# Scores of the windowed attentions: the second query tile and the doubled key rows are made on chip by ScalarE instead of being loaded

## The chip, the cores and the metric

The kernel runs on one core of a Trainium2 chip. The metric is device time in microseconds (us) of one execution. Before the change the median of three runs is 1516.51 us (1511.09 to 1520.24).

## The reference, cut to what matters

Two layers of a decoder for 1024 prompt tokens and 32 decode tokens. Layer 0 has four windowed attentions of 8 query heads on 2 key heads (kv) each: A, with a sink logit, and B in three groups with dilations 1, 4 and 16, which are merged by their softmax denominators. Each prompt attention is blocked: 128 queries read their own and the previous block of 128 keys. Layer 1 is an mLSTM and is not touched.

```python
s = jnp.einsum('nbqhgd,nbkhd->nbhgqk', qb, kk, preferred_element_type=F32)
...
p, den, lse = _softmax_stats(s, mask, sink_b)      # row maximum, exp(s - max), sums
o = jnp.einsum('nbhgqk,nbkhd->nbqhgd', p, vv.astype(F32))
o = o / jnp.moveaxis(den, -1, 2)[..., None]
```

## The kernel before

Every float32 product is made of parts: a number is split into a high part h, which TensorE multiplies at full rate, and a low part l, the rest. A projection is three matmuls (h·h, l·h and h·l, L199 to L201). For the scores the head dimension is 64 and TensorE takes 128 rows at once, so the three products fit into two matmuls: L466 multiplies the key tile K1 (128 rows: h above h) with the query tile Q1 (128 rows: l above h), and L467 adds the key tile K2 (65 rows: l, and a row of ones) with Q2 (65 rows: h, and a row with minus the softmax maximum).

The tiles are laid out for that in DRAM. `proj_q` stores a group's queries in QQ as rows l (0 to 63), h (64 to 127) and the row of minus the maximum (128), so that Q1 is rows 0 to 127 and Q2 rows 64 to 128: two loads for 256 queries of four heads, 512 KB and 260 KB (L354, L369). `proj_kv` stores keys three times in KK: h, h, l, so that K1 is 128 rows and K2 the last 64 (`k1_load`, `k2_load`). For dilations 4 and 16 a key tile is first loaded into the staging tile kt, of which there is one, and VectorE permutes it into K1 or K2 (L382, L395). Q1, Q2, K1 and K2 have two buffers each.

An attention runs in two passes over four "halves" of 256 queries. The statistics pass (`stats`, L437, L441) takes row maxima of h·h from QZ, a query tile whose lower 64 rows are zero. The score pass (`scores`) makes, block by block, two score matmuls, an exponential on ScalarE (p, L469), a mask on GpSimd, a high and a low part (ph on ScalarE, pl on VectorE or GpSimd) and three matmuls with the values (L489 to L491). There are 100 such blocks in 32 halves: 8 halves of A and 24 of B.

Work is woven: the statistics and scores of A with the projections of the other queries, the statistics of the last group and the first scores of B with the gate path (`proj_z0`), and the rest of B with the decode attention and the merges. Inside that, a scheduler at build time decides the order on each engine, which then runs it strictly in that order; on the load queue (SP) too, where an issue that waits holds back all later ones.

Of the kernel before, what the change touches and what calls it, by code (L numbers as in the profile page):

```python
# [4 lines left out]
F32 = mybir.dt.float32  # L5
F32R = mybir.dt.float32r
AF = mybir.ActivationFunctionType
# [5 lines left out]
TP, TS, T = 1024, 32, 1056  # L13
CH = ((0, 384), (384, 384), (768, 288))
DIL = (1, 1, 4, 16)
# [7 lines left out]
def f(ap):  # L23
    return ap.bitcast(F32)
# [73 lines left out]
class Builder:  # L98
# [118 lines left out]
    def proj_q(self, g):  # L217
        nc = self.nc
        dil = DIL[g]
        QQ = self.QQ[g]  # L220
        for j in range(4):
            sh = self.stage.tile([128, T], F32R, tag="sh", name="sh")
            sl = self.stage.tile([128, T], F32R, tag="sl", name="sl")
            qs = self.stage.tile([128, TS], F32, tag="qs", name="qs")

            def evac(c, t0, n, ps):
                src = ps
                if j == 3:
                    rr = self.tmp.tile([128, 384], F32, tag="rr", name="rr")
                    self.rope(rr[:, :n], ps, t0, n)  # L230
                    src = rr[:, :n]
                if c == 2:
                    nc.scalar.activation(qs, src[:, 256:288], AF.Copy, scale=0.125)  # L233
                    n = 256
                a, b = t0 // dil, (t0 + n) // dil

                def pv(ap):
                    if dil == 1:
                        return ap[:, t0:t0 + n]
                    return ap[:, :TP].rearrange("p (r n) -> p n r", r=dil)[:, a:b, :]  # L240

                s = src[:, :n]
                if dil > 1:
                    s = s.rearrange("p (n r) -> p n r", r=dil)
                self.hi(pv(sh), s, 0.125)
                self.lo(pv(sl), s, pv(sh), 0.125)

            yield from self.proj_feat(self.A['w0f'][4 + 4 * g + j], self.X0, evac)
            r0 = 128 * ((j + 1) % 4)
            self.store('q', QQ[512 + r0:640 + r0, :], f(sh[:, :TP]))  # L250
            self.store('q', QQ[r0:r0 + 128, :], f(sl[:, :TP]))
            self.store('q', self.QS[g, r0:r0 + 128, :], qs)

    def proj_kv(self):
        nc, A, O = self.nc, self.A, self.O
        tc = self.tc
        with tc.tile_pool(name="kvp", bufs=1) as kp, tc.tile_pool(name="kvt", bufs=2) as kt:
# [36 lines left out]
            for j in range(4):  # L294
                sh = self.stage.tile([128, T], F32R, tag="sh", name="sh")
                sl = self.stage.tile([128, T], F32R, tag="sl", name="sl")
                self.hi(sh[:, :TP], KF[:, j, :TP])
                self.lo(sl[:, :TP], KF[:, j, :TP], sh[:, :TP])
                r0 = 128 * ((j + 1) % 4)
                for u in range(2):  # L300
                    self.store('k', self.KK[512 * u + r0:512 * u + r0 + 128, :], f(sh[:, :TP]))
                self.store('k', self.KK[1024 + r0:1152 + r0, :], f(sl[:, :TP]))
                self.store('k', self.KS[r0:r0 + 128, :], KF[:, j, TP:T])
            wv = []
            for k in range(0, 8, 2):
# [51 lines left out]
    def qh_load(self, g, kv, hf):  # L357

        Q = self.QZ[hf % 2]
        t = slice(256 * hf, 256 * hf + 256)  # L360
        h = slice(4 * kv, 4 * kv + 4)
        self.store("Qh", f(Q[0:64]), self.QQ[g].rearrange("(d h) t -> d h t", h=8)[64:128, h, t])
        return Q

    def q2_load(self, g, kv, hf):
        Q2 = self.qp.tile([65, 4, 256], F32R, tag="Q2", name="Q2")
        t = slice(256 * hf, 256 * hf + 256)
        h = slice(4 * kv, 4 * kv + 4)
        self.load(f(Q2), self.QQ[g].rearrange("(d h) t -> d h t", h=8)[64:129, h, t])  # L369
        return Q2  # L370

    def k1_load(self, g, kv):
        nc = self.nc
        dil = DIL[g]
        src = self.KK.rearrange("(d h) t -> h d t", h=8)[2 * g + kv][0:128]
        K1 = self.kp.tile([128, TP], F32R, tag="K1", name="K1")
        if dil == 1:
            self.load(f(K1), src)
        else:
            kt = self.kp.tile([128, TP], F32, tag="kt", name="kt", bufs=1)  # L380
            self.load(kt, src)
            nc.vector.tensor_copy(K1.rearrange("p (r n) -> p n r", r=dil), kt.rearrange("p (n r) -> p n r", r=dil))  # L382
        return K1

    def k2_load(self, g, kv):
        nc = self.nc
        dil = DIL[g]
        src = self.KK.rearrange("(d h) t -> h d t", h=8)[2 * g + kv][128:192]
        K2 = self.kp.tile([65, TP], F32R, tag="K2", name="K2")
        if dil == 1:  # L390
            self.load(f(K2[0:64]), src)
        else:
            kt = self.kp.tile([128, TP], F32, tag="kt", name="kt", bufs=1)
            self.load(kt[0:64], src)
            nc.vector.tensor_copy(K2[0:64].rearrange("p (r n) -> p n r", r=dil),  # L395
                                  kt[0:64].rearrange("p (n r) -> p n r", r=dil))
        nc.gpsimd.memset(f(K2[64:65]), 1.0)
        return K2

    def v_load(self, g, kv):  # L400

# [21 lines left out]

    def stats(self, g, kv, hf, Q1, K1, ST):
        nc = self.nc
        for qb in range(2 * hf, 2 * hf + 2):
# [5 lines left out]
            for hp in range(2):  # L432
                st = self.pp.tile([128, 2, 256], F32, tag=STATS_PS[hp], name="st")
                for u in range(2):
                    h = 2 * hp + u
                    q0 = 128 * (qb % 2)
                    nc.tensor.matmul(st[:, u, :], Q1[:, h, q0:q0 + 128], K1[:, w0:w0 + 256], start=True, stop=True)  # L437
                for u in range(2):
# [14 lines left out]

    def scores(self, g, kv, hf, Q1, Q2, K1, K2, V, emit):
        nc = self.nc
# [65 lines left out]

    def attn_a(self, kv):
        nc = self.nc
        K1, K2, V = self.k1_load(0, kv), self.k2_load(0, kv), self.v_load(0, kv)
        ST = self.sm.tile([128, 32], F32, tag="ST", name="ST")
        for hf in range(4):
            Q1 = self.qh_load(0, kv, hf)
            yield from self.stats(0, kv, hf, Q1, K1, ST)
        nc.vector.tensor_tensor(ST, ST, self.sinkb[:, 32 * kv:32 * kv + 32], OP.max)
        nm = self.QQ[0][1024 + 4 * kv:1028 + 4 * kv]  # L530
        self.neg_rows(ST, nm)
        OD = self.odp.tile([65, 4, TP], F32, tag="OD", name="OD")

        def emit(qb, av):
            nc.vector.tensor_copy(self.od_view(OD, 0, qb), self.av_view(av[0:65], 0))

        for hf in range(4):
            Q1 = self.q1_load(0, kv, hf)
            Q2 = self.q2_load(0, kv, hf)
            yield from self.scores(0, kv, hf, Q1, Q2, K1, K2, V, emit)  # L540
        self.store('o', self.OD[0][kv], OD)
        self.finish(0, kv, nm)

    def attn_b_stats(self, g, kv):
        K1 = self.k1_load(g, kv)
        ST = self.sm.tile([128, 32], F32, tag="ST", name="ST")
        for hf in range(4):
            Q1 = self.qh_load(g, kv, hf)
            yield from self.stats(g, kv, hf, Q1, K1, ST)
        self.neg_rows(ST, self.NMB[kv][g - 1])  # L550
# [19 lines left out]
    def attn_b(self, kv, done=None):  # L570

        nc = self.nc
        OD = self.odp.tile([65, 4, TP], F32, tag="OD", name="OD")
        for g in (3, 2, 1):
            K1, K2, V = self.k1_load(g, kv), self.k2_load(g, kv), self.v_load(g, kv)

            def emit(qb, av, g=g):
                o = self.od_view(OD, g, qb)
                a = self.av_view(av[0:65], g)
                if g == 3:  # L580
                    for s in range(2):
                        nc.vector.tensor_copy(o[:, :, s, :], a[:, :, s, :])
                else:
                    nc.vector.tensor_tensor(o, a, o, OP.add)
                if g == 1 and qb in (2, 5, 7):
                    t = slice(CH[qb // 3][0], 128 * qb + 128)
                    self.store('o', self.OD[1][kv][:, :, t], OD[:, :, t])
                    if done:
                        done(qb // 3)

            for hf in range(4):
                Q1 = self.q1_load(g, kv, hf)
                Q2 = self.q2_load(g, kv, hf)
                yield from self.scores(g, kv, hf, Q1, Q2, K1, K2, V, emit)
        if kv == 0:
            self.finish(1, kv)
# [292 lines left out]
    def layer0(self):  # L889
        nc, tc, A, O = self.nc, self.tc, self.A, self.O  # L890
        dp = self.dram
        dt = lambda n, s: dp.tile(s, F32, name=n)
# [1 line left out]
        self.QQ = [dt(f"QQ{g}", [129 * 8, TP]) for g in range(4)]  # L894
        self.QS = dt("QS", [4, 512, TS])

        self.KK, self.KS = dt("KK", [3 * 512, TP]), dt("KSd", [512, TS])

        self.VV = dt("VV", [TP, 8 * 128])
        self.NMB = [[dt(f"NMB{i}{g}", [4, TP]) for g in range(3)] for i in range(2)]  # L900
# [722 lines left out]
```

## Time and profile before

| | |
|---|---|
| runs | 1511.09, 1516.51, 1520.24 us |
| profiled execution | 1514.5 us, of which the span of the core is 1512.8 |
| TensorE (PE) busy | 1409.6 us, 93% |
| VectorE (DVE) busy | 897.7 us, 59% |
| ScalarE (ACT) busy | 472.9 us, 31% |
| GpSimd (POOL) busy | 276.4 us, 18% |
| moved by DMA | 241.01 MB, mean 159 GB/s |
| mean granted TensorE clock | 0.971 |

The shares are averages over stages. TensorE is nearly full in the projections and in layer 1, and has its holes between 440 and 700 us, where the scores of B, the decode attention and the merges run; there the DMA engines are at their busiest. An idle engine in that table therefore says little on the stage that the change touches.

### The profile page before, as it was taken

What the parts mean: (1) busy time and instruction counts of PE and PEld (TensorE: products, weight loads), DVE (VectorE), ACT (ScalarE), POOL (GpSimd) and SP (SyncE); (2) the same over time, 40 slices, a digit from 0 to 9 for tenths busy, and PEclk for the clock granted to TensorE, in tenths of its full rate; (3) what the DMA queues carried; (4) which work ended last, traced back from release to release, by engine and by line L of the source; (5) the groups of instructions that cost most, each with busy time, mean ns of one, the idle gap of its engine ahead of it and who ended that gap; (6) DMA issues with size and microseconds to landing.
All of it is one profiled execution on the core that took longest, in us unless ns stands there. A gap on an engine that the chain in (4) does not pass through costs nothing.

```text
span 1512.8 us, 21927 instructions
## 1 busy us (share of the span) xinstructions
PE 1409.6 (93%) x7792; PEld 1193.2 (79%) x7792; DVE 897.7 (59%) x2479; ACT 472.9 (31%) x892; POOL 276.4 (18%) x351
## 2 busy tenths in 40 slices
PE   8999999999988777978999999999999999999997
PEld 7989998998887434456879878988898899877785
DVE  5311556677655856758774536555565566566786
ACT  5331143521112654512124313331333133323310
POOL 1002252512334874401000000000000000000010
PEclk9999999999999978989999999999999999999999
DMA  8646665667747998894312565364224312341731
GB/s 304 222 150 209 212 187 184 188 199 202 205 135 183 226 228 179 260 273 137 128 51 72 193 222 178 97 217 135 70 78 124 116 49 68 118 127 28 239 133 46
DMA packets 149323, 241.01 MB, mean 159 GB/s; under 512 B 17632, under 2 KB 115904, under 8 KB 148696
## 3 DMA queue, kind: packets, MB, share of 16 engines
q1 hardware_dynamic: 141150, 218.24, 49.0%
q10 hardware_dynamic: 8064, 21.37, 3.9%
q8 instruction: 62, 1.02, 0.3%
q14 instruction: 47, 0.39, 0.1%
HBM read 178.66 MB, written 83.97 MB: 174 GB/s over the span
## 4 chain that ended last, share of the span: by engine, by line
PE 67%; DMA 18%; DVE 7%; issue 3%; ACT 1%; POOL 1%; SPq 1%; DVEq 0%; POOLq 0%; ACTq 0%
PE pj L199 10%; PE pj L200 10%; PE pj L201 10%; PE py L167 3%; PE py L165 3%; PE py L166 3%; PE pvo L165 3%; PE pvo L166 3%; PE pvo L167 3%; DMA G<-GR 2%; DMA Q<-QQ 2%; DMA NMB<-NM 1%; DMA QZ<-QQ 1%; DMA OD<-OD 1%; PE av L489 1%
## 5 line engine op out<-in xcount | busy, mean ns | idle before, releaser
L199 PE MATMUL pj<-x1h,wh 128*128 128x384 f32 (+1 forms) x576 | 189.7, 329 | 1.7 <-ACT QT L1156 1.6
L199 PE MATMUL pj<-xh,wh 128*128 128x384 f32 (+1 forms) x576 | 187.9, 326 | 1.2 <-DVE rt L214 1.2
L201 PE MATMUL pj<-x1h,wl 128*128 128x384 f32 (+1 forms) x576 | 187.8, 326 | 0.0
L201 PE MATMUL pj<-xh,wl 128*128 128x384 f32 (+1 forms) x576 | 187.6, 326 | 0.0
L200 PE MATMUL pj<-xl,wh 128*128 128x384 f32 (+1 forms) x576 | 187.6, 326 | 0.0
L200 PE MATMUL pj<-x1l,wh 128*128 128x384 f32 (+1 forms) x576 | 187.6, 326 | 0.0
L199 PEld LDWEIGHTS pj<-x1h,wh 128*128 128x128 f32 x576 | 108.7, 189 | 6.5 <-issue 3.3
L201 PEld LDWEIGHTS pj<-x1h,wl 128*128 128x128 f32 x576 | 108.6, 188 | 6.0 <-issue 5.8
L199 PEld LDWEIGHTS pj<-xh,wh 128*128 128x128 f32 x576 | 109.8, 191 | 4.4 <-DVE rt L214 2.2
L200 PEld LDWEIGHTS pj<-x1l,wh 128*128 128x128 f32 x576 | 108.6, 189 | 4.0 <-issue 3.8
L201 PEld LDWEIGHTS pj<-xh,wl 128*128 128x128 f32 x576 | 110.0, 191 | 1.4
L200 PEld LDWEIGHTS pj<-xl,wh 128*128 128x128 f32 x576 | 109.6, 190 | 1.1
L441 DVE CUSTOM_DVE_ANT_0 junk<-st,maskq 128x256 f32<-128x256 f32 (+1 forms) x256 | 93.0, 363 | 25.0 <-PE st L437 5.9
L165 PE MATMUL pvo<-voh,x1h 128*128 128x512 f32 x256 | 101.7, 400 | 2.5 <-DVE SZ L1172 2.5
L166 PE MATMUL pvo<-voh,x1l 128*128 128x512 f32 x256 | 100.8, 396 | 0.0
L167 PE MATMUL pvo<-vol,x1h 128*128 128x512 f32 x256 | 100.3, 395 | 0.0
L811 POOL TENSOR_TENSOR rsw<-rsw,mhalf 128x1 f32<-128x1 f32 (+1 forms) x54 | 40.2, 745 | 321.4 <-DVE rsw L810 305.6
L122 POOL TENSOR_TENSOR wl<-wr,wh 128x1024 fp32r<-128x1024 f32 x24 | 59.2, 2470 | 122.5 <-ACT qs L233 77.8
L116 DVE TENSOR_TENSOR pl<-p,ph 128x512 fp32r<-128x512 f32 x82 | 68.3, 842 | 21.7 <-ACT ph L112 15.8
L112 ACT ACTIVATE wh<-wr 128x1024 fp32r<-128x1024 f32 x48 | 50.7, 1057 | 81.5 <-PE pj L200 75.2
L112 ACT ACTIVATE ph<-p 128x512 fp32r<-128x512 f32 x100 | 61.4, 629 | 41.6 <-PE av L490 26.2
L469 ACT ACTIVATE p<-sc 128x512 f32<-128x512 f32 x100 | 56.8, 593 | 44.6 <-PE sc L467 29.1
(349 smaller groups left out, 3145.3 us busy)
## 6 DMA issues: line engine op xcount, KB each, us to landing
Q<-QQ SPq DMA_DIRECT2D x32, 512.0 KB
out_kvs_dram<-in_cache_b_kv_dram SPq DMA_DIRECT2D x16, 1022.0 KB
wr<-in_w0f_dram SPq DMA_DIRECT2D x24, 512.0 KB
wr<-in_w1f_dram SPq DMA_DIRECT2D x24, 512.0 KB
Q<-QQ SPq DMA_DIRECT2D x32, 260.0 KB
QQ<-sh ACTq DMA_DIRECT2D x16, 512.0 KB
QQ<-sl ACTq DMA_DIRECT2D x16, 512.0 KB
QZ<-QQ SPq DMA_DIRECT2D x32, 256.0 KB
```

The lines of the kernel that those rows point to most:

```text
L112: return self.nc.scalar.activation(out, in_, AF.Copy, scale=scale)
L116: return self.nc.vector.tensor_tensor(out, in_, f(hi), OP.subtract)
L122: self.nc.gpsimd.tensor_tensor(out, in_, f(hi), OP.subtract)
L165: nc.tensor.matmul(ps, xh[:, k, t], wh, start=k == 0, stop=False)
L166: nc.tensor.matmul(ps, xl[:, k, t], wh, start=False, stop=False)
L167: nc.tensor.matmul(ps, xh[:, k, t], wl, start=False, stop=k == 7)
L199: nc.tensor.matmul(ps[:, :n], wh[:, k, :], xh[:, k, :n], start=k == 0, stop=False)
L200: nc.tensor.matmul(ps[:, :n], wh[:, k, :], xl[:, k, :n], start=False, stop=False)
L201: nc.tensor.matmul(ps[:, :n], wl[:, k, :], xh[:, k, :n], start=False, stop=k == 7)
L441: nc.vector.tensor_tensor_reduce(junk[:, :n], st[:, u, c0:c0 + n], mk, 1.0, -3e38, OP.add, OP.max, ST[:, 8 * h + qb:8 * h + qb + 1])
L469: nc.scalar.activation(p, sc, AF.Exp)
L811: nc.gpsimd.tensor_tensor(r, v, self.mhalf[:m], OP.pow)
```

## The change

1. QQ holds h in rows 0 to 63 and l in rows 64 to 127. Q1 is h above l.
2. Q2 is no longer loaded: only its row 64 (minus the maximum, 4 KB) is; rows 0 to 63 are copied by ScalarE from rows 0 to 63 of Q1, which hold h (32 copies of 64x1024).
3. KK holds h and l once each. K1's rows 0 to 63 are loaded and ScalarE copies them into rows 64 to 127 (14 copies of 64x1024, of which 6 for statistics passes). For dilations 4 and 16 one load of kt brings both parts, and VectorE permutes 64 rows into K1 and, for a score pass, 64 into K2.

```diff
-            self.store('q', QQ[512 + r0:640 + r0, :], f(sh[:, :TP]))
-            self.store('q', QQ[r0:r0 + 128, :], f(sl[:, :TP]))
+            self.store('q', QQ[r0:r0 + 128, :], f(sh[:, :TP]))
+            self.store('q', QQ[512 + r0:640 + r0, :], f(sl[:, :TP]))
...
-                for u in range(2):
-                    self.store('k', self.KK[512 * u + r0:512 * u + r0 + 128, :], f(sh[:, :TP]))
-                self.store('k', self.KK[1024 + r0:1152 + r0, :], f(sl[:, :TP]))
+                self.store('k', self.KK[r0:r0 + 128, :], f(sh[:, :TP]))
+                self.store('k', self.KK[512 + r0:640 + r0, :], f(sl[:, :TP]))
...
-        self.load(f(Q2), self.QQ[g].rearrange("(d h) t -> d h t", h=8)[64:129, h, t])
+        self.load(f(Q2[64:65]), self.QQ[g].rearrange("(d h) t -> d h t", h=8)[128:129, h, t])
+        self.nc.scalar.activation(Q2[0:64], f(Q1[0:64]), AF.Copy)
...
-    def k1_load(self, g, kv):
+    def k_load(self, g, kv, low=True):
...
+        K2 = self.kp.tile([65, TP], F32R, tag="K2", name="K2") if low else None
         if dil == 1:
-            self.load(f(K1), src)
+            self.load(f(K1[0:64]), src[0:64])
+            if low:
+                self.load(f(K2[0:64]), src[64:128])
         else:
+            n = 128 if low else 64
             kt = self.kp.tile([128, TP], F32, tag="kt", name="kt", bufs=1)
...
+            self.load(kt[:n], src[:n])
+            for u, d in enumerate((K1[0:64], K2[0:64]) if low else (K1[0:64],)):
+                nc.vector.tensor_copy(d.rearrange("p (r n) -> p n r", r=dil),
+                                      kt[64 * u:64 * u + 64].rearrange("p (n r) -> p n r", r=dil))
+        nc.scalar.activation(K1[64:128], f(K1[0:64]), AF.Copy)
+        if low:
+            nc.gpsimd.memset(f(K2[64:65]), 1.0)
+        return K1, K2
```

ScalarE's order in the scores of B, at the turn from dilation 16 to dilation 4 of the second key head, before. p is the exponential, ph the high part:

```order
L469 ACTIVATE p<-sc 128x512 x2
L112 ACTIVATE ph<-p 128x512 x3
L469 ACTIVATE p<-sc 128x512
L112 ACTIVATE ph<-p 128x512
L469 ACTIVATE p<-sc 128x512 x3
L112 ACTIVATE ph<-p 128x512 x3
```

And now, at the same turn. Q_5404, Q_5484 and Q_5805 are the Q2 tiles of three halves that follow each other, Q_5402, Q_5482 and Q_5803 their Q1 tiles, K_6019 the K1 of the group after:

```order
L465 ACTIVATE p<-sc 128x512 x3
L370 ACTIVATE Q_5404<-Q_5402 64x1024
L112 ACTIVATE ph<-p 128x512 x3
L465 ACTIVATE p<-sc 128x512 x2
L112 ACTIVATE ph<-p 128x512
L370 ACTIVATE Q_5484<-Q_5482 64x1024
L465 ACTIVATE p<-sc 128x512
L370 ACTIVATE Q_5805<-Q_5803 64x1024
L465 ACTIVATE p<-sc 128x512
L112 ACTIVATE ph<-p 128x512
L391 ACTIVATE K_6019<-K_6019 64x1024
```

Copies stand between the exponentials of earlier halves. Each waits for its half's two loads; what stands behind it on ScalarE waits too.

The load queue (SP) at the first scores of B, before (Q with 65 rows is Q2, with 128 rows Q1):

```order
L106 DMA Q_4174<-QQ_78 65x4x256
L106 DMA Q_4242<-QQ_78 65x4x256
L106 DMA wr<-in_wo_dram 128x1024
L106 DMA kt<-KK 64x1024
L106 DMA Q_4328<-QQ_78 128x4x256
L106 DMA Q_4330<-QQ_78 65x4x256
L106 DMA kt<-KK 128x1024
L106 DMA Q_4396<-QQ_78 128x4x256
```

And now:

```order
L106 DMA Q_4185<-QQ_78 1x4x256
L106 DMA Q_4254<-QQ_78 1x4x256
L106 DMA wr<-in_wo_dram 128x1024
L106 DMA kt<-KK 128x1024
L106 DMA Q_4341<-QQ_78 128x4x256
L106 DMA Q_4343<-QQ_78 1x4x256
L106 DMA Q_4410<-QQ_78 128x4x256
```

The loads keep their places; those of Q2 shrink to one row, and of the two loads of kt for a group one is left.

## Rows read from the trace of the kernel before

**Rows 1.** Busy time by stretch: PE, PEld, DVE, ACT, POOL, clock, DMA share, GB/s.

```profile
440.00:640.00 200.00, 158.97 (x692) 99.92 (x694) 133.49 (x257) 92.25 (x178) 108.61 (x132) 0.88 0.84 208
150.00:325.00 175.00, 172.00 (x1015) 159.97 (x1014) 104.74 (x282) 66.57 (x119) 63.85 (x52) 0.99 0.60 187
...
550.00:575.00 25.00, 15.94 (x41) 8.33 (x40) 9.40 (x17) 9.77 (x18) 13.46 (x27) 0.68 0.99 217
```

**Rows 2.** Waits, 440 to 640 us: who for whom, us, times, longest.

```profile
ACT p L469 <- PE sc L467: 26.0, 14, 4.8
...
DVE K L395 <- DMA kt<-KK: 12.9, 3, 5.1
...
PE sc L466 <- DMA Q<-QQ: 9.4, 5, 2.9
...
PE sc L467 <- DMA Q<-QQ: 8.8, 9, 3.4
...
DVE dn L519 <- DMA dn<-OD: 6.4, 1, 6.4
```

**Rows 3.** Chain that ended last, 435 to 600 us: start, us, what.

```profile
435.67 4.42 DMA kt<-KK
...
447.54 1.83 DMA nr<-NMB
...
469.24 4.28 DMA kt<-KK
...
481.33 4.53 DMA nr<-NMB
...
536.26 11.82 DMA Q<-QQ
...
553.11 9.79 DMA OD<-OD
562.91 12.76 DMA dn<-OD
```

**Rows 4.** DMA issues, whole span: count, KB each.

```profile
Q<-QQ SPq DMA_DIRECT2D x32, 512.0 KB
...
Q<-QQ SPq DMA_DIRECT2D x32, 260.0 KB
...
KK<-sh SPq DMA_DIRECT2D x8, 512.0 KB
...
kt<-KK SPq DMA_DIRECT2D x8, 512.0 KB
...
K<-KK SPq DMA_DIRECT2D x6, 512.0 KB
```

**Rows 5.** The same view, 480 to 640 us: packets, and loads of Q2.

```profile
DMA packets 30380, 36.33 MB, mean 227 GB/s; under 512 B 2377, under 2 KB 27127, under 8 KB 30369
...
Q<-QQ SPq DMA_DIRECT2D x20, 260.0 KB
```

**Rows 6.** ScalarE's groups by form, whole span: busy us, mean ns, idle before.

```profile
L469 ACT ACTIVATE p<-sc 128x512 f32<-128x512 f32 x100 | 56.8, 593 | 44.6 <-PE sc L467 29.1 <-DVE pl L116 12.1 <-POOL pl L485 2.3
L112 ACT ACTIVATE wh<-wr 128x1024 fp32r<-128x1024 f32 x48 | 50.7, 1057 | 81.5 <-PE pj L200 75.2 <-DMA QZ<-QQ 3.6 <-DMA wr<-in_w1f_dram 2.6
```

**Rows 7.** Timeline, 540 to 550 us: PE, then ACT: start, us, what, [idle before].

```profile
545.51 0.80 PE L466 MATMUL sc<-Q,K 128*128 128x512 f32 x1 [2.94 <-DMA Q<-QQ]
...
548.12 1.22 PE L467 MATMUL sc<-Q,K 65*128 65x512 f32 x2
...
543.04 1.08 ACT L469 ACTIVATE p<-sc 128x512 f32<-128x512 f32 x2
544.00 0.64 ACT L112 ACTIVATE ph<-p 128x512 fp32r<-128x512 f32 x1
549.44 0.60 ACT L469 ACTIVATE p<-sc 128x512 f32<-128x512 f32 x1 [4.80 <-PE sc L467]
```

More of the change, by code (lines that the diff above doesn't have):

```diff
@@ L361, in qh_load, with q2_load @@
         h = slice(4 * kv, 4 * kv + 4)
-        self.store("Qh", f(Q[0:64]), self.QQ[g].rearrange("(d h) t -> d h t", h=8)[64:128, h, t])
+        self.store("Qh", f(Q[0:64]), self.QQ[g].rearrange("(d h) t -> d h t", h=8)[0:64, h, t])
         return Q
-    def q2_load(self, g, kv, hf):
+    def q2_load(self, g, kv, hf, Q1):
         Q2 = self.qp.tile([65, 4, 256], F32R, tag="Q2", name="Q2")
@@ L368, in q2_load @@
         h = slice(4 * kv, 4 * kv + 4)
-        self.load(f(Q2), self.QQ[g].rearrange("(d h) t -> d h t", h=8)[64:129, h, t])
+        self.load(f(Q2[64:65]), self.QQ[g].rearrange("(d h) t -> d h t", h=8)[128:129, h, t])
+        self.nc.scalar.activation(Q2[0:64], f(Q1[0:64]), AF.Copy)
         return Q2
-    def k1_load(self, g, kv):
+    def k_load(self, g, kv, low=True):
         nc = self.nc
         dil = DIL[g]
-        src = self.KK.rearrange("(d h) t -> h d t", h=8)[2 * g + kv][0:128]
+        src = self.KK.rearrange("(d h) t -> h d t", h=8)[2 * g + kv]
         K1 = self.kp.tile([128, TP], F32R, tag="K1", name="K1")
+        K2 = self.kp.tile([65, TP], F32R, tag="K2", name="K2") if low else None
         if dil == 1:
-            self.load(f(K1), src)
+            self.load(f(K1[0:64]), src[0:64])
+            if low:
+                self.load(f(K2[0:64]), src[64:128])
         else:
+            n = 128 if low else 64
             kt = self.kp.tile([128, TP], F32, tag="kt", name="kt", bufs=1)
[L381 to L398, printed above, removed]
+            self.load(kt[:n], src[:n])
[6 more added lines that the diff above has]
+        return K1, K2
     def v_load(self, g, kv):
@@ L523, in attn_a @@
         nc = self.nc
-        K1, K2, V = self.k1_load(0, kv), self.k2_load(0, kv), self.v_load(0, kv)
+        (K1, K2), V = self.k_load(0, kv), self.v_load(0, kv)
         ST = self.sm.tile([128, 32], F32, tag="ST", name="ST")
@@ L538, in attn_a @@
             Q1 = self.q1_load(0, kv, hf)
-            Q2 = self.q2_load(0, kv, hf)
+            Q2 = self.q2_load(0, kv, hf, Q1)
             yield from self.scores(0, kv, hf, Q1, Q2, K1, K2, V, emit)
@@ L544, in attn_b_stats @@
     def attn_b_stats(self, g, kv):
-        K1 = self.k1_load(g, kv)
+        K1 = self.k_load(g, kv, False)[0]
         ST = self.sm.tile([128, 32], F32, tag="ST", name="ST")
@@ L574, in attn_b @@
         for g in (3, 2, 1):
-            K1, K2, V = self.k1_load(g, kv), self.k2_load(g, kv), self.v_load(g, kv)
+            (K1, K2), V = self.k_load(g, kv), self.v_load(g, kv)
             def emit(qb, av, g=g):
@@ L592, in attn_b @@
                 Q1 = self.q1_load(g, kv, hf)
-                Q2 = self.q2_load(g, kv, hf)
+                Q2 = self.q2_load(g, kv, hf, Q1)
                 yield from self.scores(g, kv, hf, Q1, Q2, K1, K2, V, emit)
@@ L895, in layer0 @@
         self.QS = dt("QS", [4, 512, TS])
-        self.KK, self.KS = dt("KK", [3 * 512, TP]), dt("KSd", [512, TS])
+        self.KK, self.KS = dt("KK", [2 * 512, TP]), dt("KSd", [512, TS])
         self.VV = dt("VV", [TP, 8 * 128])
```

## The prediction

> **What bounds the kernel now.** I read the busy time by stretch first. In the scores of A, which run beside projections, TensorE is busy 172.00 of 175 us: nothing is to be won there but by taking work from TensorE itself, and the change takes none. From 440 to 640 us, the scores of B, it is busy 158.97 of 200 us at a clock of 0.88. No other compute engine is full there: VectorE 133, GpSimd 109, ScalarE 92 of 200 us; the DMA engines stand at 0.84 over the stretch, and at 0.99 from 550 to 575, where the clock is 0.68 and ScalarE works 9.77 of 25 us [rows 1]. So the holes, 200 - 159 = 41 us, are where the change can act.
>
> Next the waits of that stretch. TensorE itself stands 9.4 + 8.8 = 18.2 us before score matmuls because a query tile has not landed: five times for Q1 (L466), nine for Q2 (L467). ScalarE in turn waits 26.0 us for L467. VectorE stands 12.9 us before a permuting copy of the second part of a key tile (L395), which needs a second load of kt, and 6.4 us before the denominators [rows 2]. The chain of waits shows what lies on the path: two loads of kt (4.42 and 4.28 us), a load of Q2 that takes 11.82 us, and, where the output tile OD passes from the first key head to the second, a store of 9.79 us and a load of the denominators of 12.76 us [rows 3]. A small transfer shows that this is largely the queue ahead of it: the 16 KB load of nr takes 1.83 us at 447.5 us and 4.53 us at 481.3 [rows 3]. The timeline shows how one late Q2 spreads: Q1's matmul starts at 545.51 after an idle 2.94 us, Q2's at 548.12, and ScalarE, done at 544.64, begins again at 549.44 [rows 7].
>
> **The change part by part.** *Bytes removed.* Each of 32 Q2 loads loses 256 of its 260 KB (8.4 MB), each of 14 K1 loads 256 KB (3.7 MB), and four of eight 512 KB stores of the high keys go (2.1 MB): 14.2 of 241 MB [rows 4]. What counts is the full stretch, 480 to 640 us: 36.33 MB at a mean of 227 GB/s. There 20 Q2 loads lose 5.2 MB and four key tiles 1.0 MB [rows 5], together 6.3 MB, 17%, or 6.3 MB / 227 GB/s = 28 us of transfer. That is the upper bound, if the transfers alone set the pace; the lower is nothing, if they run beside other work.
>
> *Waits for Q1.* Five, 9.4 us. Q1 stays 512 KB, but what is queued before it is a sixth less. A load that transits in about 6 us comes about 1 us earlier; five waits lose 1 us each: -5 us. The ends are 0 and -9.4.
>
> *Waits for Q2.* Nine, 8.8 us, the longest 3.4. Q2 is now ready when Q1 has landed and ScalarE has copied it. No row has a 64x1024 copy; the nearest is ScalarE's 128x1024 of the weights, the same 1024 elements per row, at 1057 ns [rows 6], against 593 ns for 512 elements. I take 1.06 us for a copy. In the timeline Q2 came 548.12 - 545.51 = 2.6 us after Q1 [rows 7]; a copy makes that about 1.2 us with its hand-over. Short waits stay as they are, long ones shrink: -3 us, between 0 and -8.8.
>
> *The kt wait.* For dilations 4 and 16 one load of 512 KB brings both parts, so VectorE's wait inside a group goes: 12.9 us in three, of which two, 4.42 + 4.28 = 8.7 us, lie on the chain [rows 2, 3]. What is late next is the statistics work standing there on VectorE and TensorE, and the new copy into K1's lower half, one of 1.06 us per group, behind VectorE's. I take -5 us, between 0 and -8.7.
>
> *The hand-over of OD.* 9.79 + 12.76 = 22.5 us of transfers that wait in the same queue [rows 3]. A sixth of it is 3.8 us: I take -3, between 0 and -6.
>
> *Added to ScalarE.* 32 + 14 copies of 1.06 us are 49 us in the whole span, some 25 of them (20 of Q2, four or five of K1) in the stretch, where ScalarE goes from 92 to 117 us of 200 [rows 1]. It is not full then, but the copies stand between exponentials, and each waits for two loads; behind it wait the exponentials and high parts of older blocks, behind these GpSimd's masks, VectorE's low parts and TensorE's value matmuls. Today ScalarE often stands there in any case, for the very Q loads (26.0 us) [rows 2]. I take +6 us: a quarter of the 25 us shows on the path. The ends are 0, if all of it falls into ScalarE's idle time, and +30, if every copy and half a microsecond of waiting with it does.
>
> *The rest.* The copies of A and of the statistics passes are covered by TensorE's projections, 172 of 175 us, since ScalarE has 66.57 of 175 us of work there [rows 1]; if a copy holds back the evacuation of a projection for longer than TensorE has a second PSUM buffer, a few us are lost. VectorE's permutations keep their number, 12, and I take their length as unchanged. The stores saved at the end of the key projection fall under a busy TensorE: 0. The two stores of QQ only change places: 0. Layer 1: 0.
>
> Sum: -5 - 3 - 5 - 3 + 6 = -10 us. The profiled execution took 1514.5 us (a span of 1512.8 and 1.7 around it), so 1504.5; the median of the runs is 2.0 us above the profiled one: **1506.5 us**.
>
> Here a rule of the Trainium skill speaks against the change. The 16 KB load with little ahead of it takes 1.83 us [rows 3], and the 4 KB row that is left of Q2 is such a load, for which the copy waits as well. The Trainium skill, "DMA: Bandwidth & Descriptors", section "Anatomy of one DMA — SWDGE (gpsimd) path", gives each DMA a fixed cost of about 2.0 us that does not depend on its size, for another issue path than ours; the row agrees in size. By that rule alone a shorter Q2 saves the byte part only, and its -3 us would be 0 and the sum -7.
>
> The same page, section "Why a DMA increments its semaphore by 16 and not by 1", says that a transfer uses the largest number of engines up to 16 that divides its outermost size, so 13 for the 65 rows of Q2; no row here shows a single engine. By it the old Q2 put 20 KB on each of 13 engines instead of 16 KB on 16, and Q2's late landing [rows 7] would be cured by more than its bytes: an estimate of a further -5 us.
>
> **The rivals.** *ScalarE becomes the gate (slower).* A copy is put where its loads were expected, and the loads land later than that on a busy queue; ScalarE then holds exponentials back whose scores are done. For it: in the new order the copy of Q_5805 stands before an exponential of the half two before it, when its Q1 load can hardly have been issued, because Q1 has two buffers. Against it: ScalarE idles at such places now, 4.80 us in the timeline [rows 7]. It decides from the point at which copy and hold cost more than 16 us (the sum of the gains) over the 20 halves of the stretch, 0.8 us a half. At 1.3 us a half it is 26 - 16 = +10: 1526.5 us.
>
> *The bytes were hidden.* The Q loads are late because two buffers let them be issued late, and not because of the queue; then neither Q1 nor OD comes earlier. For it: at 0.84 the DMA engines are not full over the whole stretch [rows 1]. Against it: 4.53 against 1.83 us for the same 16 KB [rows 3]. What stays is kt (-5), Q2 (-3) and ScalarE (+6): -2, so 1514.5 us.
>
> *The transfers are the pace.* If DMA sets the time from 480 to 640 us, most of the 28 us comes back, say 24, less 2 for ScalarE: -22, 1494.5 us. For it: 0.99 with a TensorE that waits at a clock of 0.68 [rows 1]. Against it: VectorE and GpSimd are busy for two thirds and more than half of the stretch, and ScalarE gets 25 us more.
>
> **How the numbers follow.** The forecast has 0.35, the pace of transfers 0.13, hidden bytes 0.28, ScalarE as the gate 0.24. What a measurement here can tell from no change is 0.5%, 7.6 us: faster is below 1508.9, slower above 1524.1. Forecast and transfer pace make faster, 0.47, with a little of the forecast's spread given to no change; hidden bytes make no change, 0.29; the gate makes slower, 0.24. The forecast's own range is 1500 to 1513 us. The range reaches down towards the transfer pace, 1491, and up to the middle of the gate's case, 1527.
>
> **What would show it.** Right: between 440 and 640 us the DMA share or the stretch's length falls, TensorE's waits for Q drop from 18.2 to under 12 us, VectorE's wait for kt is gone, the chain loses its long Q load, and ScalarE's copies take 1.0 to 1.1 us and start mostly without a wait. Wrong: the copies show waits for DMA of more than a microsecond each, the waits of p and ph for copies or of L467 for ScalarE reach the 18.2 us that went, or TensorE's busy time from 150 to 325 us falls, since ScalarE evacuates the projections too late.

## The result and the profile after

The changed kernel takes 1495.82 us (median of 4 runs, 1493.39 to 1500.81) against 1517.68 us (1511.09 to 1520.24) for the kernel before: a ratio of 0.987, 95% interval 0.982 to 0.991. It is faster by 1.3%, some 20 us, twice the 10 us forecast: inside the forecast's whole range, 1491 to 1527 us, but below its own narrower one, 1500 to 1513. The profiled execution took 1500.81 us, its span 1499.1.

Busy time by stretch, the answers to [rows 1], columns as there:

```profile
440.00:640.00 200.00, 169.06 (x804) 107.29 (x803) 146.07 (x276) 121.70 (x214) 111.44 (x133) 0.89 0.63 183
150.00:325.00 175.00, 170.39 (x1006) 158.76 (x1005) 103.08 (x270) 76.92 (x129) 61.90 (x53) 0.99 0.54 168
550.00:575.00 25.00, 18.82 (x54) 9.84 (x54) 14.38 (x26) 18.58 (x31) 17.32 (x32) 0.76 0.58 167
```

TensorE does 10 us more work in the 200 us of B, the DMA share falls from 0.84 to 0.63, and ScalarE rises from 92 to 122 us. The stretch that stood at a DMA share of 0.99 stands at 0.58. In A, TensorE is busy 1.6 us less than its 172.0. From 480 to 640 us the transfers, to compare with [rows 5] (packets; then loads by size):

```profile
DMA packets 24983, 30.82 MB, mean 193 GB/s; under 512 B 2192, under 2 KB 21852, under 8 KB 24972
...
Q<-QQ SPq DMA_DIRECT2D x20, 512.0 KB
...
Q<-QQ SPq DMA_DIRECT2D x20, 4.0 KB
```

The waits from 440 to 640 us, which answer to [rows 2] (engine and line that waits, for whom; us, times, longest):

```profile
DVE pl L116 <- ACT ph L112: 16.3, 12, 6.3
ACT Q L370 <- DMA Q<-QQ: 14.0, 9, 3.4
PEld av L485 <- ACT ph L112: 13.4, 14, 4.6
...
PE av L485 <- ACT ph L112: 8.6, 6, 4.2
...
PE sc L462 <- DMA Q<-QQ: 4.1, 2, 2.5
ACT p L465 <- PE sc L463: 4.1, 6, 1.3
...
DVE K L389 <- DMA kt<-KK: 0.9, 1, 0.9
...
PE sc L463 <- DMA Q<-QQ: 0.7, 1, 0.7
```

Three rows of the same view of the kernel before, which were not needed until now:

```profile
PEld av L489 <- ACT ph L112: 7.0, 6, 3.3
...
DVE pl L116 <- ACT ph L112: 3.8, 5, 1.2
...
PE av L489 <- ACT ph L112: 2.0, 2, 1.3
```

Read together, they show the direction of waiting turned round. Before, ScalarE stood 26.0 us for the score matmuls and TensorE 18.2 us for Q. Now TensorE stands 4.8 us for Q and ScalarE 4.1 us for scores, but ScalarE stands 14.0 us ahead of the copies, and VectorE and TensorE stand for ScalarE's high parts (line 112): 16.3 against 3.8 us, 13.4 against 7.0, 8.6 against 2.0. GpSimd's wait for the high parts went the other way, from 14.7 to 10.6 us. Of VectorE's wait for kt, 12.9 us, 0.9 are left. The timeline shows how one copy holds the others back (first ScalarE, then TensorE; start, us, what, [idle before]):

```profile
529.47 0.58 ACT L465 ACTIVATE p<-sc 128x512 f32<-128x512 f32 x1
532.23 1.06 ACT L370 ACTIVATE Q<-Q 64x1024 fp32r<-64x1024 f32 x1 [2.18 <-DMA Q<-QQ]
533.19 0.58 ACT L465 ACTIVATE p<-sc 128x512 f32<-128x512 f32 x1
533.67 0.62 ACT L112 ACTIVATE ph<-p 128x512 fp32r<-128x512 f32 x1
...
533.82 0.50 PE L462 MATMUL sc<-Q,K 128*128 128x512 f32 x1 [1.03 <-ACT p L465]
```

At 532.23 the copy begins, after a wait of 2.18 us for its query tile, and an exponential stands behind it until 533.19; TensorE's next score matmul starts at 533.82, after 1.03 us of waiting for an exponential.

The chain from 440 to 640 us, to compare with [rows 3] (start, us, what):

```profile
450.21 1.82 DMA nr<-NMB
...
489.20 5.41 DMA K<-KK
494.63 1.06 ACT K L391
...
542.61 6.08 DMA Q<-QQ
...
557.92 5.47 DMA OD<-OD
```

The long load of Q has become 6.08 us, the store of OD 5.47 instead of 9.79, and the load of the denominators is no longer on it. The copies' length is as taken (ScalarE's groups, columns as in [rows 6]):

```profile
L465 ACT ACTIVATE p<-sc 128x512 f32<-128x512 f32 x100 | 56.1, 588 | 10.6 <-PE sc L463 6.2 <-POOL pl L481 2.3 <-DVE pl L116 1.7
L370 ACT ACTIVATE Q<-Q 64x1024 fp32r<-64x1024 f32 x32 | 33.7, 1055 | 38.2 <-DMA Q<-QQ 31.9 <-DVE ST L437 6.2
L391 ACT ACTIVATE K<-K 64x1024 fp32r<-64x1024 f32 x14 | 14.8, 1058 | 30.7 <-DVE K L389 17.3 <-DMA K<-KK 13.2
```

To set kernels side by side, I laid the matmul records of each trace together, from the start of the span to the last matmul of layer 0's output projection ("busy" is the union of their times, "idle" the rest). What follows that point, layer 1, takes 733 to 738 us in every kernel. "Scores of B" is the time from its first to its last score matmul, "tail" from there to the end of that projection:

| kernel | to the end of layer 0 | busy | idle | scores of B | tail |
|---|---|---|---|---|---|
| before | 775.4 | 698.7 | 76.7 | 165.7 | 143.5 |
| after | 761.2 | 694.6 | 66.6 | 154.0 | 138.0 |
| query part alone | 761.1 | 692.3 | 68.7 | 156.4 | 136.4 |
| key part alone | 753.3 | 690.6 | 62.6 | 157.7 | 131.0 |
| key part + 24 copies | 780.7 | 701.5 | 79.3 | 154.2 | 156.4 |
| after + each copy twice | 781.3 | 701.4 | 79.8 | 167.4 | 140.0 |
| after + bytes back | 775.2 | 706.5 | 68.7 | 151.7 | 147.4 |

Each row is one execution, and executions of one kernel lie up to 20 us apart: those of the changed kernel and of the query part alone took the longest of their kernel's, those of the key part alone, of each copy twice and of the bytes back the shortest. So a difference of a few us between two rows is not a finding. The rows also differ by up to nine of some 3780 matmul records.

After against before: 10.1 us less idle, and 4.1 us less busy, for the same matmuls. The score stage gains 11.7 us and the tail 5.5. The first statistics matmul begins 4.3 us later (173.4 against 169.1 us). The copy of K1 is not the reason: it is done at 113.9 us. The store of the queries that these statistics load is issued 4.2 us later already, at 163.42 instead of 159.21 us; why, is open.

### The profile page after: what moved, and what is told of

It reads as the page before. It is cut to its first block, busy times and chain, and to the rows that moved or that the text cites. A ratio compares the mean times of both kernels' runs of the same rounds, so it can differ in the third digit from the quotient of the medians.

```text
span 1499.1 us, 21984 instructions
## 1 busy us (share of the span) xinstructions
PE 1405.4 (94%) x7792; PEld 1191.7 (79%) x7792; DVE 901.5 (60%) x2479; ACT 515.1 (34%) x938; POOL 276.0 (18%) x351
## 4 chain that ended last, share of the span: by engine, by line
PE 69%; DMA 16%; DVE 8%; issue 3%; ACT 2%; POOL 2%; SPq 1%; DVEq 0%; ACTq 0%; POOLq 0%
PE pj L199 10%; PE pj L201 10%; PE pj L200 10%; PE py L165 4%; PE py L167 3%; PE py L166 3%; DMA G<-GR 3%; PE pvo L165 3%; PE pvo L166 3%; PE pvo L167 3%; DMA wr<-in_wo_dram 1%; PE st L433 1%; DMA QZ<-QQ 1%; DMA out_cmems_dram<-Cs 1%; PE sc L463 1%
## 5 line engine op out<-in xcount | busy, mean ns | idle before, releaser
L437 DVE CUSTOM_DVE_ANT_0 junk<-st,maskq 128x256 f32<-128x256 f32 (+1 forms) x256 | 93.1, 364 | 27.4 <-PE st L433 6.8
L1198 POOL MEMSET V<- 128x2 f32 x64 | 4.3, 99 | 348.6 <-PE num L1327 213.9
```

What stands on the lines that cost most here:

```text
L437: nc.vector.tensor_tensor_reduce(junk[:, :n], st[:, u, c0:c0 + n], mk, 1.0, -3e38, OP.add, OP.max, ST[:, 8 * h + qb:8 * h + qb + 1])
```

## Experiments

Ratios are to the kernel before, with 95% intervals; a difference in us is that of two ratios times 1515 us. The kernels ran on more than one chip, and each is compared with runs of the kernel before on its own. A difference to the changed kernel is uncertain by 7 to 8 us, since that kernel's own ratio is known to 0.0043; one to the key part alone by 5 us. The theory was that the gain is bytes taken from the full stretch, less the copies on ScalarE. The rivals: that the gain is in the waits and the order of work (kt, OD, the tail), and the bytes were hidden; and that the copies cost nothing.

**The query part alone.** Q2's copy and its one-row load, with the keys loaded and stored as before.

```
 def q2_load(self, g, kv, hf, Q1):
-        self.load(f(Q2), ...[64:129, h, t])
+        self.load(f(Q2[64:65]), ...[128:129, h, t])
+        self.nc.scalar.activation(Q2[0:64], f(Q1[0:64]), AF.Copy)
```

> Kernel before with the query part alone: Q2's 64 rows copied by ScalarE, keys as before. Bytes theory (the load queue sets the pace of the scores of B, so a time falls with the bytes taken out of it): Q2 is 5.2 of the 6.3 MB that go from 480 to 640 us, so 17 of the 21 us that the change gained, about 1500 us against 1517. Key theory (VectorE's wait for the second load of kt, 12.9 us, was the loss): this kernel still has two loads of kt, so it gains under 5 us, 1513 or more.

Measured: 0.9874 (0.9849 to 0.9899), 19 us less than before, as much as the whole change, and near the 17 us of the bytes theory; the key theory's limit of 5 us is passed.

**The key part alone.** One load of kt, keys stored once, 14 copies of K1; Q2 is loaded whole.

```
+        (K1, K2), V = self.k_load(g, kv), self.v_load(g, kv)
 ...
         self.load(f(Q2), ...[64:129, h, t])
```

> Kernel before with the key part alone: keys stored once, K1's lower half copied by ScalarE, one load of kt; Q2 loaded with 65 rows as before. Bytes theory: 1.0 of 6.3 MB, about -4 us, 1513 us. Key theory: the wait of VectorE for kt goes, -8 us or more, 1509 us or less.

Measured: 0.9855 (0.9833 to 0.9878), 22 us less, with no copy of Q. Here the bytes theory, with 4 us, fails; the key theory, with 8 us or more, holds. Each part alone is worth about 20 us, and both together 20 as well. So making Q2 by a copy gains 19 us in the kernel before and nothing once the key part is in; this set the next questions.

**Bytes back.** The changed kernel, with a transfer of 256 KB per half from the queries in DRAM to a scratch tensor there, issued ahead of Q2's row; nothing waits for its data.

```
+        self.load(self.JK[8 * g + 4 * kv + hf], self.QQ[g]...[0:64, h, t])
```

> Kernel after with the 256 KB that Q2 no longer loads moved all the same: a transfer of the same 64 rows from QQ to a scratch tensor in DRAM, issued on the load queue ahead of Q2's row, which nothing waits for. Bytes theory: 5.2 MB are back in the queue between 470 and 630 us, so the gain of Q goes: 1512 to 1520 us. Theory that bytes do not matter, but that Q2's own landing was the wait (it is a copy now): stays within 4 us of the kernel after, 1496 to 1500 us.

Measured: 1.0030 (1.0012 to 1.0048): 25 us slower than the changed kernel. All that was won is lost again, by 8.4 MB that no instruction reads, and by the 32 issues that move them. Where it is lost is not where I looked: the scores of B take 151.7 us, no longer than after, but the stage begins at 476.1 instead of 469.2 us, and the tail takes 9.4 us more. The stretch of the scores, first after, then with the bytes back, is no fuller:

```profile
480.00:640.00 160.00, 131.42 (x583) 71.55 (x582) 121.36 (x187) 111.66 (x198) 104.94 (x125) 0.87 0.67 193
```

```profile
480.00:640.00 160.00, 127.56 (x476) 63.64 (x475) 112.15 (x178) 110.93 (x197) 107.64 (x131) 0.83 0.66 196
```

ScalarE waits no longer for Q ahead of its copies either (440 to 640 us, against 14.0 us in nine):

```profile
ACT Q L371 <- DMA Q<-QQ: 14.5, 10, 3.7
```

So the run shows an amount, and not that full DMA engines in the scores are the way it is lost. The table has 14 of the 25 us, 12 of them as busy time; the clock explains 7.6 of these (last section). What a further issue in the load queue costs by itself was not measured apart.

**Q2's load in two.** The kernel before, 64 rows and one row apart.

```
-        self.load(f(Q2), ...[64:129, h, t])
+        self.load(f(Q2[0:64]), ...[64:128, h, t])
+        self.load(f(Q2[64:65]), ...[128:129, h, t])
```

> Kernel before with Q2's load of 65 rows split in two loads, 64 rows and 1 row; bytes and everything else as before. Bytes theory: no change, 1514 to 1521 us. Shape theory (a load of 65 rows is spread over fewer of the 16 DMA engines than one of 64 and therefore lands late): Q2 lands earlier, TensorE's waits for Q fall, 1503 to 1509 us.

Measured: 0.9950 (0.9924 to 0.9976), 8 us less, with every byte still moved, as the shape theory had it; a run further down, with the same edit in another kernel, speaks against it.

**Each copy twice.** The changed kernel with a second, identical copy right behind the first.

```
+        self.nc.scalar.activation(Q2[0:64], f(Q1[0:64]), AF.Copy)
```

> Kernel after with each copy of Q1 into Q2 made twice in a row on ScalarE: 32 more copies of 1.06 us, 24 of them in the scores of B. Theory that ScalarE's copies cost on the path what the load saves (the two halves of the change gain 19 and 22 us alone and 20 together, so some 20 us are eaten): a copy costs about its length, 15 to 25 us, 1511 to 1521 us. Theory that ScalarE's idle time hides them and something else is the floor: under 6 us, 1496 to 1502 us.

Measured: 1.0093 (1.0068 to 1.0118), 34 us (26 to 42) slower than the changed kernel for 32 more copies. ScalarE's groups in this kernel show what the second one is:

```profile
L370 ACT ACTIVATE Q<-Q 64x1024 fp32r<-64x1024 f32 x32 | 33.7, 1054 | 40.3 <-DMA Q<-QQ 35.8 <-DVE ST L438 4.4
L371 ACT ACTIVATE Q<-Q 64x1024 fp32r<-64x1024 f32 x32 | 33.6, 1049 | 0.2
```

The second copy waits for nothing (0.2 us idle before all 32) and is 33.6 us long; the kernel is 34 us longer, if by ratios, and 20 us between the two traces in the table. That the two lengths agree so well is chance, but a copy does cost about its length, and by no means a quarter of it, on an engine that is busy for about two thirds of the stretch.

**The copy on VectorE.** The changed kernel, Q2 copied there instead.

```
-        self.nc.scalar.activation(Q2[0:64], f(Q1[0:64]), AF.Copy)
+        self.nc.vector.tensor_copy(Q2[0:64], f(Q1[0:64]))
```

> Kernel after with the copy of Q1 into Q2 on VectorE instead of ScalarE. Theory of ScalarE as the price: ScalarE is relieved of 24 copies in the scores of B, 5 to 15 us faster than the kernel after, 1481 to 1491 us, if VectorE has the room (58 of 80 us busy, as ScalarE). Theory that an in-order engine that waits for a load is the price, whichever it is: within 5 us of the kernel after or slower.

Measured: 0.9901 (0.9884 to 0.9919). That is 5 us above the changed kernel, so the same within the uncertainty: not better than on ScalarE. VectorE, too, stands in the loop from scores to values, with the low parts, and waits for the same loads ahead of its copies (8.6 us in four, 440 to 640 us).

**Another order, nothing else.** The kernel before with one weight of the weave changed, to see what a mere shift of the order is worth.

```
-W1, W2, W3, W4 = (129, 76), (86, 80), (28, 15, 6), (64, 90)
+W1, W2, W3, W4 = (129, 76), (86, 95), (28, 15, 6), (64, 90)
```

> Kernel before with nothing changed but a weight of the weave between the gate path and the scores of B (80 becomes 95), which gives another order of the same instructions. If the gains of the parts are those of the order they happen to get, this can move as far, 8 us or more either way. If not, it stays within 5 us of the kernel before, 1510 to 1520 us.

Measured: 1.0014 (0.9989 to 1.0039). This one shift is worth nothing. But it is a small one. Every edit makes the scheduler find another order: counted by the longest order common to both, about 35 of some 3780 matmuls of layer 0 stand elsewhere here, against 329 from before to after, 229 for the copies added to the key part, 340 and 361 for each copy twice and the bytes back. What such a shift costs by itself was not measured, so it may have a part in every difference here.

**The weights of the output projection on another queue.** The changed kernel, layer 0's loads of wo issued by GpSimd, so that they don't stand behind SP's waits.

```
-        self.load(raw, src[:, k, :])
+        (self.load if self.layer else self.nc.gpsimd.dma_start)(raw, src[:, k, :])
```

> Kernel after with the eight loads of the output projection's weights issued on GpSimd's queue instead of behind the other loads of SP. In the kernels so far the last of these weights is split 86 to 93 us before the end of the projection, whatever came before. Theory that their place in SP's order sets the time between the last score and the projection: they come earlier, 3 to 8 us faster than after, 1488 to 1493 us. Theory that the transfers themselves are the limit there (0.99 of the engines from 640 to 660 us): no change, within 3 us.

Measured: 0.9939 (0.9917 to 0.9961), 11 us slower than the changed kernel: neither theory's number. The weights did not come earlier in its trace, either: the last of them is split 74 us after the last score matmul, against 73 in the changed kernel. So the run doesn't tell what earlier weights would be worth, and the 11 us are unexplained.

**The key part with copies that nothing reads.** This takes the change apart in two steps: key part plus copies, then the bytes of Q2.

```
                 Q2 = self.q2_load(g, kv, hf, Q1)
+                nc.scalar.activation(self.QZ[hf % 2][0:64], f(Q1[0:64]), AF.Copy)
```

> The key part alone (measured 0.9855 of before) with one ScalarE copy of 64x1024 added in each of the 24 halves of B, out of Q1 into a tile that nothing reads; Q2 is still loaded whole, so no byte goes. It takes the whole change apart in two steps: key part + copies, then copies + fewer bytes. Theory A (a copy stands on the path at about its whole length, 24 x 1.06 = 25 us, and the whole change then gets these back through the 6.3 MB that Q2 no longer loads): ratio 1.000 to 1.005. Theory B (both parts relieve the same queue, and after the first nothing is left to gain; the copies fall into ScalarE's idle time): as the key part alone, 0.984 to 0.988. Between: 0.992, each counts for half.

Measured: 1.0039 (1.0016 to 1.0062). The 24 copies cost 1.84% or 28 us (23 to 33) against the key part alone, 1.2 us each, as theory A had it; the changed kernel, which has such copies, eight more in A and only a row of Q2 to load, is 26 us (19 to 33) faster than this one. The two steps share this run, and since the key part alone and the whole change are equally fast, they must be equal; each has a second run of its own above, 34 and 25 us. Busy time by stretch, the key part alone and then with the copies:

```profile
480.00:640.00 160.00, 129.45 (x515) 73.83 (x513) 116.07 (x180) 91.11 (x168) 96.63 (x116) 0.85 0.86 227
640.00:750.00 110.00, 104.12 (x580) 80.41 (x580) 88.04 (x171) 19.78 (x31) 10.61 (x11) 0.97 0.53 175
```

```profile
480.00:640.00 160.00, 127.43 (x476) 74.02 (x475) 113.36 (x157) 108.36 (x183) 109.47 (x125) 0.83 0.78 198
640.00:750.00 110.00, 91.99 (x519) 67.42 (x518) 77.12 (x152) 22.47 (x43) 8.21 (x8) 0.89 0.64 212
```

The scores themselves run no longer with the copies (154.2 against 157.7 us), yet TensorE gets through 476 matmuls instead of 515: what the weave puts beside the scores is what falls behind, and it is done in the tail, which is 25 us longer. Of the 27.4 us that the table shows to the end of layer 0, about 16.7 are idle and 10.9 are the same work at a lower clock. The waits from 440 to 640 us, again the key part alone and then with the copies:

```profile
ACT p L464 <- PE sc L462: 17.6, 14, 3.7
...
DVE pl L116 <- ACT ph L112: 10.9, 8, 2.8
```

```profile
DVE pl L116 <- ACT ph L112: 23.0, 15, 7.7
ACT QZ L589 <- DMA Q<-QQ: 20.7, 12, 3.5
...
ACT p L464 <- PE sc L462: 2.2, 4, 0.9
```

These waits of ScalarE did not go, they changed their name: of 17.6 us ahead of exponentials 2.2 are left, and 20.7 us stand ahead of copies. There, at twelve places, a copy can't lie in the idle time; it begins when the wait for Q1 ends, and the exponentials come after it. That the exponentials had waited for the same load, through the score matmuls, is shown in part only: in the key part's trace TensorE waited for a load of Q ahead of three of the 14, 8.5 of the 17.6 us. And it is not the whole account: ScalarE is busy 17 us more in these 160 us, so its idle time as a whole did shrink, and the kernel became longer all the same.

**The key part with Q2's load in two.** The one split that had helped, on the better half.

```
-        self.load(f(Q2), ...[64:129, h, t])
+        self.load(f(Q2[0:64]), ...[64:128, h, t])
+        self.load(f(Q2[64:65]), ...[128:129, h, t])
```

> The key part alone with the load of Q2 in two, 64 rows and one row; ScalarE copies nothing of Q. On the kernel before this split was worth 0.995. Theory A (Q2's landing is still on the path, TensorE waits 17 us for Q loads in the key part's stretch): 0.979 to 0.983, faster than both kernels. Theory B (the key part has taken what the queue had to give): 0.984 to 0.988.

Measured: 0.9973 (0.9952 to 0.9994), 18 us slower than the key part alone: neither theory's number. The trace shows 13.7 us more idle of TensorE (76.3 against 62.6) and waits of SP's queue for loads of Q (430 to 640 us):

```profile
SPq L106 <- DMA Q<-QQ: 15.4, 11, 3.2
```

In the key part alone that wait is 8.5 us, in the split of the kernel before 6.3, in the next kernel, with the same split, 5.0. So it doesn't explain the loss by itself; why the same edit gains 8 us in one kernel and loses 18 in another is open. That the order changes with it, 332 of some 3780 matmuls as counted above, is a rival that no run excludes.

**Statistics over 64 rows.** As the kernel before this one, and six copies of K1 less.

```
-  nc.tensor.matmul(st[:, u, :], Q1[:, h, q0:q0 + 128], K1[:, w0:w0 + 256], ...)
+  nc.tensor.matmul(st[:, u, :], Q1[0:64, h, q0:q0 + 128], K1[0:64, w0:w0 + 256], ...)
 ...
+        if low:
-        nc.scalar.activation(K1[64:128], f(K1[0:64]), AF.Copy)
+            nc.scalar.activation(K1[64:128], f(K1[0:64]), AF.Copy)
```

> As the run before it, and the statistics matmuls contract over 64 rows and not 128 (the lower 64 rows of the query tile there are zero), so that the six key tiles that only statistics use need no copy into their lower half: six ScalarE copies of 1.06 us fewer, two of them behind the load of keys of the last group that stands on the chain. Theory A (a copy on the path costs its length): 2 to 4 us less than the run before it, 0.002 lower. Theory B (covered by projections): the same within 0.002.

Measured: 0.9984 (0.9965 to 1.0003), the same as the run before it. It doesn't settle what K1's copies cost, because the edit brought a price of its own; windows of the run before it, then of this one:

```profile
325.00:400.00 75.00, 65.66 (x408) 61.76 (x407) 47.99 (x180) 15.11 (x24) 17.60 (x13) 1.00 0.73 204
```

```profile
325.00:400.00 75.00, 75.00 (x397) 60.24 (x395) 50.98 (x193) 13.84 (x23) 14.88 (x10) 1.00 0.65 184
```

TensorE is busy all the time at the same clock and does fewer matmuls; more on this in the last section.

**Q1's load in two.** The changed kernel, the rows that are copied first.

```
-        self.load(f(Q1), ...[0:128, h, t])
+        self.load(f(Q1[0:64]), src[0:64, h, t])
+        self.load(f(Q1[64:128]), src[64:128, h, t])
```

> The changed kernel with the load of Q1 in two of 256 KB, the rows that ScalarE copies first. ScalarE waits 14.0 us for these loads at nine copies between 430 and 630 us in the changed kernel. Theory A (the wait ahead of a copy is what it costs, more than its length): the copy begins 1 to 2 us earlier in each of 20 halves, 10 to 15 us less than the changed kernel, 0.977 to 0.980. Theory B (its length and place in ScalarE's order are what it costs; the row of the last load and the extra issues give the rest back): 0.985 to 0.990, as the changed kernel.

Measured: 0.9954 (0.9926 to 0.9981), 13 us (5 to 21) slower than the changed kernel. ScalarE's wait ahead of the copies did not shrink, it grew (430 to 640 us):

```profile
ACT Q L372 <- DMA Q<-QQ: 27.3, 14, 4.4
```

against 14.0 us in nine: neither theory's number. A smaller load was not an earlier one here, so the wait could not be taken away in this manner, and its share of a copy's price was not measured.

No version beats both kernels by more than the intervals: the key part alone (0.9855) and the whole change (0.9867) are the same.

## Why the prediction came out as it did

The direction held, and the signs of all terms; the size was half of what came, because three terms were far too small. The copies cost some 28 us and not 6, the bytes of Q2 gave about as much back and not 8, and the key part gave 22 and not the 8 of kt and OD together. That the first two nearly cancel was luck: with either of them alone so large the time would have left the range. And the parts don't add: copies for bytes is worth 19 us in the kernel before and nothing on the key part, which no term foresaw and no run explains.

*Waits for Q* (-5 and -3). The sign came as forecast: TensorE's 18.2 us fell to 4.8, below the 12 named. But waits that are seen at one engine were too small a measure of what Q2's bytes were worth. Two experiments give it: 8.4 MB of Q2 taken away, copies kept, is worth 26 us; 8.4 MB put back costs 25. The 20 loads in the full stretch are 5.2 MB, at 227 GB/s 23 us [rows 5], which is the same size, as the rival with 0.13 had it. That the transfers were the pace of that stretch is not shown by this: with the bytes put back its DMA share is 0.66 and the scores are no longer, and the key part alone gains 22 us with 1.0 MB less in it, under 5 us at 227 GB/s. That rival's time, 1494.5 us, is near the measured one, but not for its reason: it allowed 2 us for ScalarE.

*Added to ScalarE* (+6). This is the step that failed: "a quarter of the 25 us shows on the path". About all of it shows, 28 us for 24 copies and 34 us for 32. The rival of ScalarE as the gate had the mechanism and nearly the price, 26 us over 20 halves; it lost because the gains that it set against it, 16 us, were too small. The 26.0 us of idle time in which I let the copies hide [rows 2] were misread, too: I put them down to "the very Q loads", but the trace shows TensorE waiting for a load of Q ahead of only four of the 14, 11.2 us; ahead of others, such as the 4.6 us up to 630.38, it was busy with value matmuls and the decode attention. Where Q was the reason, a copy waits for it as well. The signs were mixed: 13 of the 23 copies from 440 to 640 us start without a wait, a sign of being right, and six wait for Q for more than a microsecond each, 14.0 us at nine in all, a sign of being wrong.

*The kt wait* (-5). It fell from 12.9 us to 0.9 in the stretch, and the key part as a whole is worth 22 us net of its 14 copies; how much of that is kt, the hand-over of OD and the 5.8 MB of keys that are no longer moved is not taken apart.

*The hand-over of OD* (-3). On the chain, the store went from 9.79 to 5.47 us, and the denominators' load, 12.76 us, left it. I had allowed for the transfers' sixth, 3.8 us of the two; the chain shows more, but what that is worth was not measured apart.

*The rest* (0). Layer 1 is unchanged, 737.4 against 737.8 us. The copies of A were covered but for 1.4 us of idle (1.9 to 3.3 us between the first statistics matmul and the last score of A). Not in the sum were the later start of the statistics (4.3 us) and the 4.1 us less of busy time, of which the clock explains under 1 us (last section). Nor was the tail, 5.5 us: in the run with 24 copies, work that is put beside the scores came back there.

*The rule that spoke against.* The 4 KB row did not turn the copy's gain to nothing: TensorE waits 0.7 us at line 463 for it, once. The Trainium skill, "DMA: Bandwidth & Descriptors", section "Anatomy of one DMA — SWDGE (gpsimd) path", has a fixed cost of about 2 us for each DMA on another path; the 16 KB load at 1.82 us again agrees with that, and the sum of -7 that I derived was farther off than the one I took.

*The 65 rows.* Splitting off the odd row gained 8 us in the kernel before and lost 18 in the key part alone. The same page's section "Why a DMA increments its semaphore by 16 and not by 1" would have the 64 rows on all 16 engines in both; the first run agrees with it, the second doesn't, and no run shows a single engine.

What is open: the price of K1's copies, the key part's gain by its pieces, and why further splits of loads cost 13 to 18 us and another queue for the weights 11, why the two parts don't add, and how much of each difference is the new order that every edit brings.

## What to carry to other kernels

Idle time of an in-order engine is room for a new instruction only if that instruction is ready before the idle time ends: here 24 copies, half of which waited for the same loads as the work behind them, cost about their whole length. Where a stretch runs with the DMA engines at 0.9 and more, price the bytes at its GB/s as well as by the waits that one engine shows, and then test it: for Q2 this came to 23 us and the experiments to 25, for the keys to under 5 and the experiment to 22. When two halves of a change gain the same as both together, add the suspected cost alone to the better half, with no data behind it; that run gave the size of both terms. And where a scheduler finds a new order for every edit, test its size with shifts as large as those that the experiments bring.

## What the runs showed of the hardware

A change between matmuls over 128 and over 64 contracted rows cost time. With the statistics over 64 rows, a statistics matmul itself is as long as over 128 (both answers: min/median/max ns; first and last start; form), first over 128 rows:

```profile
L433 PE MATMUL st<-K,QZ x256: 274/281/579, 170.7 to 480.6; 128*128 128x256 f32 x128
```

```profile
L433 PE MATMUL st<-K,QZ x256: 271/278/387, 174.4 to 492.4; 64*128 64x256 f32 x128
```

But from one start to the next, the median between 170 and 490 us went from 174 to 268 ns (projection to statistics), from 123 to 223 (statistics to statistics), and from 117 to 207 (statistics to projection): about 0.1 us more at each of these steps. It is paid around the change: most statistics matmuls stand in pairs, and where more than two follow each other, the steps from the second on have a median of 118 ns (27 steps), as over 128 rows. Nor does every change of the number cost it: in the scores the step from the matmul over 128 rows to the one over 65 has a median of 234 ns in the kernel after (180 to 760 us), that between two over 128 rows, of the same 512 columns, 231 ns. The stage up to B's first score became 12 us longer (493.4 against 481.6 us), though TensorE stood still for less of it.

And a stall can cost more than its own length where the clock falls with it: the copies on the key part cost 16.7 us of idle time and 10.9 us of busy time for the same matmuls, at a granted clock of 0.83 and 0.89 in the two stretches shown instead of 0.85 and 0.97. Up to the end of layer 0, TensorE is busy at the lower of its two levels, 1.2 GHz, for 79.1 us with them and 53.1 without. The same matmuls take about half as long at the other level, 2.4 GHz: in the kernel after, score matmuls start 0.43 us apart at 526 us and 0.23 at 532, where the granted clock is 0.50 and 1.00. So these 26 us more are some 13 us of added time, enough for the 10.9. Elsewhere the clock explains less. The second copy cost 13.2 us of idle and 6.8 of busy time, with 4.2 us more at the lower level, or 2.1 us; the bytes put back 2.1 of idle and 11.9 of busy time, with 15.2 us more, or 7.6; and the 4.1 us of busy time that the change itself saved go with 1.3 us less, or 0.7. The rest is open.
